# Six buffers for split weights, each 32 bytes further round a 128-byte block than the one before it

## Chip, cores and metric

The kernel runs on one core of one Trainium2 chip. The metric is device time in microseconds (us), the median of repeated executions. The engines are named as the profile names them: PE is TensorE (PEld its weight loads), DVE is VectorE, ACT is ScalarE, POOL is GpSimd, SP is SyncE.

## What is computed

Two transformer blocks of one sequence, 256 tokens by 1024 features, in float32. Cut to its calls:

```python
def reference(...):
    x = first_block(x, c, w_ada, ..., w_in, ..., w_branch, w_out, w_up, conv_w, conv_b, w_down)
    return second_block(x, gla_w_in_2, ..., gla_w_out_2, w_kv_2, swa_w_in_2, swa_w_out_2, ...)
    # first_block: modulation by c @ w_ada; three attention branches on h @ w_in, gated and
    #   merged through w_branch and w_out; conv FFN: gelu(conv(h @ w_up)) * gate, @ w_down
    # second_block: a gated linear attention layer (w_in, w_out), then shared keys and values
    #   (w_kv) and dilated window attention (swa_w_in, swa_w_out); layer norms around them
```

Nearly all the work is a product of a 256-row activation with a weight matrix of 1024 or more rows, and each weight is read from memory once.

## The kernel before

**Split weights.** A float32 product is made of three matmuls in the faster format float32r (`mm3`, L267): each operand is a high part and a low part, and low x high, high x low and high x high are added up. Activations are split where they are made. Weights are split as they arrive, by the class `Stream` (L100). It holds the list of all weight chunks in the order of their use. For each chunk one DMA of up to 128 x 2048 floats goes into one of three `raw` buffers (L144). Then, for each half of 1024 columns, ACT copies it in rounded form into `whi` (L154) and DVE subtracts that from the raw half into `wlo` (L155). There are six `whi` and six `wlo` buffers (HLB, L26), 4096 bytes in each partition, so three chunks' worth. `get` (L164) issues the chunk that is wanted and two more (LOOK). A buffer comes free when the last matmul on its half has read it.

**How the matmuls use them.** Most products (`wstat`, L512, called by `wpair`, L517; `branch`, L751) load 128 x 128 of the weights as the stationary operand and stream the activation's 256 columns. Products by token (`tokmm`, L793) do it the other way round: 128 tokens of the activation are loaded, and 512 columns of the weights stream. The engines' orders come out of a scheduling framework that keeps dependencies and gives a tile a buffer of its tag; `high_priority` and `issue_after` steer it.

**Placing.** `Lines` (L203) wraps a pool: a tile of less than 128 bytes goes into a separate small pool, and any other is rounded up to a multiple of 128 bytes, so that all larger tiles begin at the same place in a block of 128 bytes. The pool `wp` holds `raw`, `whi` and `wlo`; `cn` holds constants and long-lived tiles, among them `rbc` (L485, one value for each token, used by `first_h`, L411, in the first stage alone); `p0` is the pool of the first stage, closed at L504.

**Order around the weights.** In the list (L276 to L318) the branch weights `br` come between the gate weights `zg`: `("br", 2)`, `("zg", 11)`, then `("out", 0)` to `("out", 3)`. The second half of `("br", 2)` is still read after the matmuls of `("zg", 11)` (`branch2`, L755, called with 2 and 3 at L790), while `out` is already being fetched and split. `swa_scores` (L1248) keeps row statistics in `sst`, a small tile with four buffers, for each of its 16 blocks of 128 queries.

Of the kernel before, what the change touches and what calls it, by code (L numbers as in the profile page):

```python
# [8 lines left out]
F32 = mybir.dt.float32  # L9
F32R = mybir.dt.float32r  # L10
# [8 lines left out]
S = 256  # L19
# [6 lines left out]
RAWB, HLB, LOOK, LASTF = 3, 6, 2, 4  # L26
# [73 lines left out]
class Stream:  # L100


    def __init__(self, nc, pool, rawbufs, hlbufs, look):
        self.nc, self.pool, self.rawbufs, self.hlbufs, self.look = nc, pool, rawbufs, hlbufs, look
        self.items = []
        self.done = []
        self.pos = 0
        self.idx = {}
        self.behind = ()
        self.after = {}  # L110
        self.later = []
        self.pri = 0

    def also(self, key, ap, fn):

# [16 lines left out]
    def _chunk(self, i):  # L132
        nc = self.nc
        key, ap, n, part = self.items[i]
        if part < 0:
            raw = self.early.tile([128, n], F32, tag="early", name="early", bufs=3)
        else:
            raw = self._raw()
        if not part:
            for o in range(0, n, 1024):  # L140
                nc.sync.dma_start(raw[:, o:o + 1024], ap[:, o:o + 1024])
            self.done.append(raw)
            return
        nc.sync.dma_start(raw[:, :n], ap)  # L144
        parts = []
        for o in range(0, n, part) if part > 0 else range(0, -part, 1024):
            m = min(part, n - o) if part > 0 else min(1024, -part - o)
            hi = self.pool.tile([128, 1024], F32R, tag="whi", name="whi", bufs=self.hlbufs)
            lo = self.pool.tile([128, 1024], F32R, tag="wlo", name="wlo", bufs=self.hlbufs)
            with ExitStack() as st:  # L150
                for ins in self.behind:
                    st.enter_context(self.tc.issue_after(ins))
                st.enter_context(self.tc.high_priority(self.pri))
                i0 = nc.scalar.activation(hi[:, :m], raw[:, o:o + m], AF.Copy)  # L154
                i1 = nc.vector.tensor_sub(lo[:, :m], raw[:, o:o + m], hi[:, :m].bitcast(F32))  # L155
                self.last = (i0.ins, i1.ins)
            parts.append((hi, lo))
        self.done.append((part, parts) if part > 0 else (raw, (1024, parts)))
# [68 lines left out]
def hybrid_blocks(ctx, tc, A, out, dbg=None):  # L227
# [3 lines left out]
    cn = Lines(ctx.enter_context(tc.tile_pool(name="cn", bufs=1)), sm)  # L231
    wp = Lines(ctx.enter_context(tc.tile_pool(name="wp", bufs=1)))
    ps = ctx.enter_context(tc.tile_pool(name="ps", bufs=1, space=PSUM))

    def open_pool(name):
        st = ExitStack()
        p = st.enter_context(tc.tile_pool(name=name, bufs=1))
        return Lines(p, st.enter_context(tc.tile_pool(name=name + "s", bufs=1))), st.close

    p1a, close_p1a = open_pool("p1a")  # L240
    p0, close_p0 = open_pool("p0")
# [8 lines left out]
    def at_t():  # L250
        return ps.tile([128, 512], F32, tag="at", name="at", bufs=2)
# [5 lines left out]
    def mm(o, l, r, start, stop, share=False):  # L257
        return pe.matmul(o, l, r, start=start, stop=stop, skip_group_check=share)  # L258
# [16 lines left out]

    ws = Stream(nc, wp, RAWB, HLB, LOOK)  # L276
    ws.tc = tc
    for j in range(KK):
        ws.add(("ada", j), A["w_ada1"][j], 2048, 0)
        ws.add(("in1", j), A["w_in1"][j], 2048, -1536)  # L280
# [201 lines left out]
    pr = at_t()  # L482
    for b in range(2):
        mm(pr[:, b * 128:(b + 1) * 128], r1[:, b:b + 1].to_broadcast([128, 128]), ident, True, True)
    rbc = cn.tile([128, S], F32, name="rbc")  # L485
    dve.tensor_copy(rbc, pr[:, 0:S])
    h32, at = first_h(0, ga)
    for j in range(KK):
# [17 lines left out]
    wk = p1  # L506
# [396 lines left out]
    wk = p2  # L903
# [64 lines left out]
    wk = p3  # L968
# [245 lines left out]
    wk = p4  # L1214
# [33 lines left out]
    def swa_scores(h):  # L1248

        kv, q = h // 4, sq[h]  # L1250
        r = []
        for b in range(2):
            bs = slice(b * 128, (b + 1) * 128)
            pl = at_t()
            mm(pl[:, 0:256], q[:, 0, bs], skT[:, 0 + kv, :], True, True)
            mm(pl[:, 256:384], q[:, 1, bs], skT[:, 2 + kv, bs], True, True)
            mm(pl[:, 384:512], q[:, 2, bs], skT[:, 4 + kv, bs], True, True)
            P = wk.tile([128, 512], F32, name="sP", tag="sP", bufs=2)
            st = wk.tile([128, 4], F32, name="sst", tag="sst", bufs=4)
            dve.tensor_tensor_reduce(P, pl, swam[:, b, :], 1.0, -3e38, OP.add, OP.max, accum_out=st[:, 0:1])  # L1260
            dve.tensor_scalar(st[:, 1:2], st[:, 0:1], -SC_SWA, None, op0=OP.mult)
            act.activation(P, P, AF.Exp, scale=SC_SWA, bias=st[:, 1:2], accum_out=st[:, 2:3])
            dve.reciprocal(st[:, 3:4], st[:, 2:3])
            dve.tensor_scalar(P, P, st[:, 3:4], None, op0=OP.mult)
            r.append(P)
        return r
# [37 lines left out]
    for h in range(8):  # L1304
        if h < 7:
            swa_q0(h + 1)
        if h in (2, 4, 6):
            swa_pv(h // 2 - 1)
        if h == 7:
            pe = Queue(tc, pe, last_mm)  # L1310
            tokmm(y4, [(sact[3], 0, w, 1024)], 1024, False, False)
        Ps = swa_scores(h)
        if h == 2:
            lnb0 = row("lnb0", nc.scalar)
            x3p = p4.tile([128, 2, D], F32, name="x3p")
            x3v = x3d.rearrange("b p d -> (b p) d").rearrange("(i b a) d -> a b i d", b=4, a=4)
            for a in range(4):
                for b in range(4):
                    q = (a % 2) * 64 + b * 16
                    nc.scalar.dma_start(x3p[q:q + 16, a // 2, :], x3v[a, b])  # L1320
        if h == 6:
            lnr = row("lng1", nc.scalar), row("lnb1", nc.scalar)
        if h in (4, 5):
            dve.tensor_add(x3p[:, h - 4, :], x3p[:, h - 4, :], lnb0)
        if h < 7:
            swa_q1(h + 1)
        if h in (2, 6):
            w = ws.get(("sout", h // 4))
            for u in range(2 - h // 4):
                tokmm(y4, [(sact[h // 4 * 2 + u], 0, w, u * 1024)], 1024, h == 2 and u == 0, False)  # L1330
        if h < 7:
            swa_tr(h, Ps)
# [106 lines left out]
```

## Time and profile before

| What | Value |
|---|---|
| Median of 3 runs | 745.18 us |
| Lowest, highest | 742.55, 747.92 us |
| The profiled execution: its time | 743.82 us |
| its span, first to last instruction | 741.8 us |
| its mean granted clock of TensorE | 0.979 |
| Instructions | 12192 |
| PE busy | 711.8 us (96%) |
| DVE, ACT busy | 547.3 us (74%), 407.8 us (55%) |
| Moved by DMA | 148.74 MB, mean 201 GB/s |

The span runs from the first to the last instruction; some 2 us of the execution lie around it. A busy matmul engine is not one at its peak, since matmuls overlap; so the distance between their starts matters as well as their durations. The granted clock is the share of 2.4 GHz that TensorE was given, 0.50 being 1.2 GHz.

### The profile page before, as it was taken

The numbers are of one execution on the slowest core, as the hardware profiler recorded it, in microseconds if no ns is written. First come the engines' busy times: TensorE is split into PE (matmuls) and PEld (weight loads), VectorE is DVE, ScalarE is ACT, GpSimd is POOL, SyncE is SP. The second block draws the span as 40 slices with busy tenths as digits, with TensorE's granted clock in tenths as the row PEclk, the third lists the DMA queues.
The fourth block names the chain that finished last, engine by engine and source line by source line (L and its number), as shares of the span: only waits on it lengthen the run. The fifth ranks groups of instructions, "written<-read, shape, count | busy, mean of one in ns | idle before, by whom it ended". The sixth has DMA issues, their size and how long they took to land. (4 is left out here: it accounts for less than half of the span.)

```text
span 741.8 us, 12192 instructions
## 1 busy us (share of the span) xinstructions
PE 711.8 (96%) x4878; PEld 649.1 (88%) x4878; DVE 547.3 (74%) x933; ACT 407.8 (55%) x675; POOL 20.2 (3%) x34
## 2 busy tenths in 40 slices
PE   4999999999979999999999999999989999999995
PEld 4888888998869999998999797888879999999984
DVE  5877969898868676758655756675877679677866
ACT  3447788546548455554454685343555556555542
POOL 0001000000010000000000200001010000000000
PEclk8999999999998999999999999999999999999999
DMA  8995767567634764658545454331447755433201
GB/s 313 421 350 204 291 255 296 204 240 274 243 142 171 266 246 171 243 204 307 211 179 191 142 220 171 115 114 57 166 160 253 259 189 180 158 128 131 97 1 57
DMA packets 24600, 148.74 MB, mean 201 GB/s; under 512 B 2992, under 2 KB 3248, under 8 KB 9568
## 3 DMA queue, kind: packets, MB, share of 16 engines
q1 hardware_dynamic: 21888, 139.05, 51.1%
q0 software_dynamic: 1280, 5.18, 2.1%
q10 hardware_dynamic: 1376, 3.74, 1.5%
q8 instruction: 38, 0.62, 0.3%
q14 instruction: 18, 0.15, 0.1%
HBM read 145.86 MB, written 2.10 MB: 199 GB/s over the span
## 5 line engine op out<-in xcount | busy, mean ns | idle before, releaser
L155 DVE TENSOR_TENSOR wlo<-raw,whi 128x1024 fp32r<-128x1024 f32 (+1 forms) x193 | 231.4, 1210 | 67.7 <-ACT whi L154 67.6
L154 ACT ACTIVATE whi<-raw 128x1024 fp32r<-128x1024 f32 (+1 forms) x193 | 199.4, 1050 | 95.8 <-PE acc L258 41.7
L258 PE MATMUL mm<-h2hi,wlo 128*128 128x256 f32 x352 | 100.2, 286 | 0.0
L258 PE MATMUL mm<-h2hi,whi 128*128 128x256 f32 x352 | 100.0, 285 | 0.0
L258 PE MATMUL mm<-h2lo,whi 128*128 128x256 f32 x352 | 97.3, 283 | 0.0
L258 PE MATMUL mm<-x3hi,wlo 128*128 128x256 f32 x304 | 87.9, 290 | 0.0
L258 PE MATMUL mm<-x3hi,whi 128*128 128x256 f32 x304 | 87.0, 287 | 0.0
L258 PE MATMUL mm<-x3lo,whi 128*128 128x256 f32 x304 | 83.7, 283 | 0.0
L258 PEld LDWEIGHTS mm<-h2hi,wlo 128*128 128x128 f32 x352 | 68.5, 194 | 0.3
L258 PEld LDWEIGHTS mm<-h2hi,whi 128*128 128x128 f32 x352 | 68.4, 194 | 0.0
L258 PEld LDWEIGHTS mm<-h2lo,whi 128*128 128x128 f32 x352 | 66.5, 192 | 0.4
L258 PE MATMUL mm<-hhi,wlo 128*128 128x256 f32 x208 | 60.9, 293 | 0.0
L258 PE MATMUL mm<-hhi,whi 128*128 128x256 f32 x208 | 60.4, 291 | 0.0
L258 PE MATMUL mm<-hlo,whi 128*128 128x256 f32 x208 | 60.1, 289 | 0.0
L258 PEld LDWEIGHTS mm<-x3hi,wlo 128*128 128x128 f32 x304 | 59.2, 195 | 0.2
L258 PEld LDWEIGHTS mm<-x3hi,whi 128*128 128x128 f32 x304 | 59.2, 195 | 0.0
L258 PEld LDWEIGHTS mm<-x3lo,whi 128*128 128x128 f32 x304 | 57.4, 192 | 0.0
L258 PEld LDWEIGHTS mm<-hhi,wlo 128*128 128x128 f32 x208 | 40.6, 195 | 1.8 <-issue 0.9
L258 PEld LDWEIGHTS mm<-hlo,whi 128*128 128x128 f32 x208 | 40.6, 195 | 0.8 <-issue 0.8
L258 PEld LDWEIGHTS mm<-hhi,whi 128*128 128x128 f32 x208 | 40.5, 195 | 0.6 <-issue 0.5
L440 DVE SCALAR_TENSOR_TENSOR adacc<-raw,cact,adacc 128x1024 f32<-128x1024 f32 x28 | 35.7, 1275 | 0.2
L258 PE MATMUL acc<-whi,flo 128*128 128x512 f32 x88 | 34.8, 395 | 0.0
(355 smaller groups left out, 1609.8 us busy)
## 6 DMA issues: line engine op xcount, KB each, us to landing
raw<-in_w_up_dram SPq DMA_DIRECT2D x22, 1024.0 KB, 4.8
raw<-in_w_ada_dram SPq DMA_DIRECT2D x16, 1024.0 KB, 4.8
raw<-in_swa_q_dram SPq DMA_DIRECT2D x16, 1024.0 KB, 4.9
raw<-in_w_zg_dram SPq DMA_DIRECT2D x12, 1024.0 KB, 5.2
raw<-in_w_dn_dram SPq DMA_DIRECT2D x11, 1024.0 KB, 4.8
raw<-in_w_ada_dram SPq DMA_DIRECT2D x16, 512.0 KB, 8.6
early<-in_w_in_dram SPq DMA_DIRECT2D x8, 1024.0 KB, 7.5
raw<-in_gla_vg_dram SPq DMA_DIRECT2D x8, 1024.0 KB, 4.9
```

The costliest lines, as they stand in the source:

```text
L154: i0 = nc.scalar.activation(hi[:, :m], raw[:, o:o + m], AF.Copy)
L155: i1 = nc.vector.tensor_sub(lo[:, :m], raw[:, o:o + m], hi[:, :m].bitcast(F32))
L258: return pe.matmul(o, l, r, start=start, stop=stop, skip_group_check=share)
L440: dve.scalar_tensor_tensor(a, w, c, a, op0=OP.mult, op1=OP.add)
```

## The change

The six buffers of the high parts become six tags with one buffer each, `whi0` to `whi5`, likewise `wlo0` to `wlo5`, and a counter `made` gives them out in turn. Ahead of everything else in `wp`, a loop allocates for each tag its buffer and behind it a pad of four floats, past the rounding of `Lines`. Two further edits give space: `rbc` moves from `cn` to `p0`, and `sst` has three buffers instead of four.

```diff
@@ class Stream
-        self.pri = 0
+        self.pri = self.made = 0
@@ _chunk
-            hi = self.pool.tile([128, 1024], F32R, tag="whi", name="whi", bufs=self.hlbufs)
-            lo = self.pool.tile([128, 1024], F32R, tag="wlo", name="wlo", bufs=self.hlbufs)
+            j = self.made % self.hlbufs
+            self.made += 1
+            hi = self.pool.tile([128, 1024], F32R, tag=f"whi{j}", name="whi")
+            lo = self.pool.tile([128, 1024], F32R, tag=f"wlo{j}", name="wlo")
@@ hybrid_blocks
     ws.tc = tc
+    for part in ("whi", "wlo"):
+        for j in range(HLB):
+            wp.pool.tile([128, 1024], F32R, tag=f"{part}{j}", name="home")
+            wp.pool.tile([128, 4], F32, tag=f"{part}pad{j}", name="pad")
@@
-    rbc = cn.tile([128, S], F32, name="rbc")
+    rbc = p0.tile([128, S], F32, name="rbc")
@@ swa_scores
-            st = wk.tile([128, 4], F32, name="sst", tag="sst", bufs=4)
+            st = wk.tile([128, 4], F32, name="sst", tag="sst", bufs=3)
```

## Rows read from the trace of the kernel before

**Rows 1.** The page, part 1: busy us (share of the span) x instructions.
```profile
PE 711.8 (96%) x4878; PEld 649.1 (88%) x4878; DVE 547.3 (74%) x933; ACT 407.8 (55%) x675; POOL 20.2 (3%) x34
```

**Rows 2.** Windows: us, busy of PE, PEld, DVE, ACT, POOL; clock; DMA.
```profile
223.50:417.00 193.50, 192.09 (x1342) 179.84 (x1341) 133.87 (x183) 101.30 (x149) 2.21 (x4) 0.99 0.58 210
...
550.00:712.00 162.00, 161.97 (x1230) 156.27 (x1229) 125.23 (x216) 96.03 (x152) 1.13 (x2) 0.99 0.48 167
```

**Rows 3.** Waits of PE: us in total, times, longest; first and last of twelve.
```profile
PE acc L885 <- DVE x L189: 4.1, 3, 2.7
...
PE at L690 <- ACT Pat L674: 0.2, 1, 0.2
```

**Rows 4.** Waits of all engines: us in total, times, longest; those of the splits.
```profile
DVE wlo L155 <- ACT whi L154: 68.1, 71, 2.7
...
ACT whi L154 <- PE acc L258: 41.7, 36, 3.1
```

**Rows 5.** Timeline of PE at 300 and 200 us: start, duration, instruction.
```profile
300.10 0.28 PE L258 MATMUL mm<-h2lo,whi 128*128 128x256 f32 x1
...
301.06 0.28 PE L258 MATMUL mm<-h2hi,wlo 128*128 128x256 f32 x1
...
199.68 0.39 PE L258 MATMUL acc<-whi,mlo 128*128 128x512 f32 x1
...
201.94 0.39 PE L258 MATMUL acc<-wlo,mhi 128*128 128x512 f32 x1
```

**Rows 6.** Timeline of PE shortly after 224 us, eight starts apart.
```profile
224.19 0.41 PE L258 MATMUL mm<-h2hi,wlo 128*128 128x256 f32 x1
...
225.90 0.41 PE L258 MATMUL mm<-h2hi,wlo 128*128 128x256 f32 x1
```

**Rows 7.** Windows as above: granted clock at 224 us and at 300 us.
```profile
223.60:225.00 1.40, 1.40 (x8) 1.40 (x7) 1.40 (x4) 1.40 (x5) 0.00 (x0) 0.50 0.00 0
...
300.00:301.20 1.20, 1.20 (x13) 1.20 (x12) 1.20 (x2) 0.00 (x0) 0.00 (x0) 1.00 0.10 41
```

**Rows 8.** Timeline of PE's weight loads: one at 300 us; eight behind one another.
```profile
300.10 0.19 PEld L258 LDWEIGHTS mm<-h2hi,whi 128*128 128x128 f32 x1
...
461.79 0.97 PEld L258 LDWEIGHTS at<-Xq,Xk 128*128 128x128 f32 x8
```

**Rows 9.** Windows, whole span: tile whi (PE, PEld, DVE, ACT), then tile wlo (without ACT).
```profile
0.00:741.80 741.80, 573.31 (x2720) 444.72 (x2720) 245.96 (x209) 211.94 (x209) 0.98 0.55 201
...
0.00:741.80 741.80, 422.16 (x1360) 263.21 (x1360) 245.96 (x209) 0.98 0.55 201
```

**Rows 10.** Groups by form, DVE: count | busy us, mean ns | idle before.
```profile
L935 DVE SCALAR_TENSOR_TENSOR u<-mm,cols,u 128x255 f32<-128x255 f32 x22 | 10.6, 483 | 16.4 <-ACT u L934 16.3
...
L189 DVE SCALAR_TENSOR_TENSOR h2lo<-acc,sh,h2hi 128x256 fp32r<-128x256 f32 x8 | 3.2, 477 | 1.7 <-ACT h2hi L189 1.7
```

**Rows 11.** Tile whi, ACT: duration min/median/max, first and last start; whole, 225 to 230.5.
```profile
L154 ACT ACTIVATE whi<-raw x193: 833/1058/1107, 63.0 to 711.4; 128x1024 fp32r<-128x1024 f32 x185, 128x768 fp32r<-128x768 f32 x8
...
L154 ACT ACTIVATE whi<-raw x5: 1098/1100/1107, 225.6 to 229.4; 128x1024 fp32r<-128x1024 f32 x5
```

**Rows 12.** Timelines of ACT and PE around the start of the product by w_out.
```profile
188.43 1.06 ACT L154 ACTIVATE whi<-raw 128x1024 fp32r<-128x1024 f32 x1 [2.67 <-PE mm L258]
...
195.04 1.04 ACT L154 ACTIVATE whi<-raw 128x1024 fp32r<-128x1024 f32 x1
...
194.54 0.28 PE L258 MATMUL mm<-yhi,whi 128*128 128x256 f32 x1
```

**Rows 13.** Tiles rbc and sst: duration min/median/max in ns, first and last start.
```profile
L413 DVE TENSOR_TENSOR xT<-xT,rbc x8: 414/418/425, 15.9 to 22.9; 128x256 f32<-128x256 f32 x8
...
L1260 DVE DVE_READ_ACCUMULATOR2_ANT sst<- x16: 80/83/85, 605.0 to 719.3; 128x1 f32 x16
...
L1264 DVE TENSOR_SCALAR sP<-sP,sst x16: 477/487/491, 607.8 to 720.6; 128x512 f32<-128x512 f32 x16
```

## Prediction

> **What bounds the kernel now.** I read the page's first part, then busy time by stage, then the waits, then the matmuls one by one. TensorE (PE) is busy 711.8 of the 741.8 us [rows 1]. In the two long stages it is busy 192.09 of 193.50 us and 161.97 of 162.00 us [rows 2], so there the time is simply the number of matmuls times the distance from one start to the next; I call that distance the pitch. What PE does wait for is short: twelve rows from 4.1 us down to 0.2 us, and in none does a matmul wait for a high or low part of the weights [rows 3]. The splitting engines stand the other way round: the ScalarE (ACT) split that makes `whi` waits for PE to give a buffer back, 41.7 us in 36 waits behind one kind of matmul, and the VectorE (DVE) split that makes `wlo` waits for ACT [rows 4]. The buffers are full and their makers idle. So the change moves the end only through the pitch, or through a wait that it creates.
>
> **The pitch.** At 300 us eight matmuls of 256 columns start in 301.06 - 300.10 = 0.96 us: 120 ns each. Ten of 512 columns start in 201.94 - 199.68 = 2.26 us: 226 ns [rows 5]. The 256 further columns cost 106 ns, so a matmul costs about 13 ns besides its columns. Shortly after 224 us, where the granted clock is 0.50 (the 1.2 GHz level; it is 1.00, 2.4 GHz, at 300 us [rows 7]), eight of the same 256-column matmuls take 225.90 - 224.19 = 1.71 us, 214 ns each [rows 6]. That is 2 x 107, with no 13 ns on top. So at full clock the 13 ns belong to a step ahead of the array that does not halve with its clock: getting an operand started, by all that can be seen. A weight load starts in the same hundredth of a us as the matmul before it, at 300.10 [rows 5, 8]. Where loads set the pace, eight in a row, the pitch is (0.97 - 0.19)/7 = 111 ns [rows 8]. Under a 256-column matmul a load therefore has 120 - 111 = 9 ns of cover.
>
> **The change, part by part.**
>
> *Six tags and pads instead of one tag.* Nothing is executed for the homes and pads; no instruction is added or removed. A pad of four floats follows each home, and if it takes 32 bytes the high parts lie at 0, 32, 64, 96, 0, 32 bytes in a block of 128, and the low parts, six pads further on, at 64, 96, 0, 32, 64, 96. Before, `Lines` rounds every row to 128 bytes and all lie at 0. Twelve pads are 384 bytes, three blocks, so `raw`, allocated behind them, keeps its place in a block, and no DMA changes.
>
> *DVE on shifted buffers.* The trace has a near case: L935 works on `u` shifted by 4 bytes, 255 columns in 483 ns, while the aligned `h2lo` with the same kind of pointer operand takes 477 ns for 256 [rows 10]. A shift costs at most some 6 ns; on 209 low splits that is 1.3 us, on an engine whose splits nobody waits for. Cost 0; 1.3 us if all of it were exposed.
>
> *ACT on shifted buffers.* The trace shows no shifted ACT split. From below: the 1024-column split has a median of 1058 ns, and five run to 1098 to 1107 ns between 225.6 and 230.5 us, where DVE splits beside it [rows 11]. If that is two engines in the same place of a block, the shift gives back 5 x 45 ns = 0.2 us there. From above: one split 50 ns longer each time is 209 x 0.05 = 10.5 us of ACT time, spread over an engine that stands waiting for buffers 41.7 us behind one releaser alone [rows 4]. Both ends are hidden by the full buffers: 0. If that cover were gone, the 10.5 us would count.
>
> The Trainium skill, "SBUF — State Buffer", section "Who interferes with whom", says that only the port pair shared by VectorE and GpSimd causes contention and that PE and ACT wait for nobody. By that rule, staggering has nothing to give. The slow ACT splits beside DVE [rows 11] do not fit it well; by the rule the sum is 0, by those rows 0.2 us off the path.
>
> *PE on shifted buffers.* 2720 matmuls use `whi` and 1360 `wlo` [rows 9]. `tokmm` uses the weights as the moving operand: 12 matmuls for each half of out (8), dn (22), gvg (16), gout (8), kvv (8) and sout (8), 70 halves, 840 matmuls, 560 on `whi` and 280 on `wlo`. The other 4080 - 840 = 3240 load them as the stationary operand (2160 and 1080). By the offsets 4 of 6 `whi` and 5 of 6 `wlo` buffers leave place 0: 373 + 233 = 606 moving and 1440 + 900 = 2340 stationary matmuls. No row shows one on a buffer off place 0, so bounds. From above: a shifted operand pays one more start of 13 ns. Moving: 606 x 13.3 = 8.1 us. Stationary: 13.3 ns less 9 ns of cover, 4.3 ns, x 2340 = 10.1 us. From below: if the 13 ns are a collision of the load and the stream starting together at the same place, the shift removes it: 9 ns (down to the loads' 111) x 2340 = 21.1 us and 8.1 us of the moving. I take 0: the 13 ns are the same for a short and a long stream [rows 5], which is how a fixed start looks, and a stream and a load that read at different rates pass each other's place in the block wherever they begin.
>
> *Fixed turns.* One tag gave a tile whichever slot came free; six tags force strict turns. They differ in one place. The second half of out1 comes six halves after the second half of br2, which is read until 194.54 us; before, its split ran at 188.43 us, so it sat in another slot [rows 12]. Now it must wait until about 194.8 us, some 6 us later, changing places with the split at 195.04. Queued behind it on ACT and DVE are only the splits of out2. PE reaches that half after 34 more matmuls of 226 ns, at 194.7 + 7.7 = 202.4 us; split there by 195.04 + 1.06 + 1.22 = 197.3 us, it is 5 us early. `raw` of out1 comes free 6 us later too, for a weight that is not needed before 223 us. Cost 0; with the cover gone, 6 us less 5, about 1 us.
>
> *`rbc` moved, `sst` from 4 to 3.* `rbc` has its last of eight reads at 22.9 us [rows 13], long before `p0` closes after the first stage. The 16 score blocks are spread from 605.0 to 719.3 us, about 7 us each, and `sst` is last read by L1264, 2.8 us after its block's start [rows 13]; a slot used again three blocks later never waits. Cost 0.
>
> **Sum.** 0 on the profiled execution's 743.82 us (span 741.8 and 2.0 around it). That execution lies 1.4 us below the median of the three runs, 745.18, well inside their 742.55 to 747.92. I forecast the median: 745.2 us.
>
> **Rivals.**
>
> *A shifted operand costs PE a start (slower).* Place: moving weights first, from `out` to the last `sout`. Price: 745.2 + 8.1 = 753.3 us, and 763.4 us with the stationary 10.1 us. It decides once a shifted load grows by over 9 ns, or a shifted stream at all. For: PE has no slack [rows 2], so any of it shows in full. Against: nothing in the trace shows PE at odds with an address. The same page of the Trainium skill, section "Specifications (TRN2)", puts the penalty on crossing 16-byte lines; by that rule a shift by a multiple of 32 crosses no more of them, and this rival gives 745.2 us.
>
> *Collision relieved (faster).* 745.2 - 29.2 = 716.0 us, if the 13 ns are a collision between the load and the stream, or part of that. For: both begin at the same instant at the same place [rows 5, 8]. Against: the reasons above.
>
> *A new wait at out1.* 745.2 + 1 us at most: within no change.
>
> *It does not do what it says.* If a pad takes a whole block, all buffers stay at place 0, only the turns change: 745.2 us, 5 in 100, within no change.
>
> **How the numbers follow.** A run of this kernel can tell about 1% from no change, 737.7 to 752.6 us. Zero by rows everywhere, with the new wait and the empty change: 63 in 100. The shifted start: 22 in 100, about two thirds of it at 753 to 758 (moving operands, or part of the loads). The relieved collision: 15 in 100. A range from 738 to 758 us leaves out most of the faster case and the upper third of the slower, some 2 in 10; the likeliest case's own range is 741 to 750 us. Faster 0.15, same 0.63, slower 0.22.
>
> **What would show it.** If right: pitches of 120 and 226 ns as before, loads 111 ns apart where they set the pace, PE about 712 us busy, the split of out1's second half near 195 us with no PE wait behind it, ACT splits at 225 us no longer near 1.1 us or unchanged, with no effect either way. The slower rival shows a pitch near 240 ns in `tokmm`, on some buffers and not on others; the faster one a pitch near 111 ns. Wrong would be any PE wait for `whi` or `wlo`, or splits so long that the buffers run empty.

## The result and the profile after

The changed kernel takes 753.76 us (median of 4 runs, 751.94 to 758.5); the kernel before, timed beside it, 745.1 us (4 runs, 742.55 to 747.92). The ratio is 1.0135, with a 95% interval of 1.0104 to 1.0165: slower by a little over 1%. The profiled execution took 753.55 us, of which the span is 751.5 us; before, the span was 741.8 us.

The page of the changed kernel, part 1 (busy us, share of the span, instructions), answers to [rows 1]:

```profile
PE 711.3 (95%) x4878; PEld 646.7 (86%) x4878; DVE 547.6 (73%) x933; ACT 408.2 (54%) x675; POOL 20.1 (3%) x34
```

Taken together, the work itself did not get longer. Every engine has the instruction counts of before, and PE is busy 711.3 us against 711.8 (the pitches did move, in both directions; see below). So the 9.7 us of longer span are time in which PE waits. The waits of PE after (engine, line and tile that wait, what for: us in total, times, longest) answer to [rows 3]:

```profile
PE acc L891 <- DVE x L191: 7.3, 3, 4.7
PE acc L891 <- DVE xr L191: 4.4, 1, 4.4
...
PE mm L260 <- DVE st L678: 3.5, 1, 3.5
...
PE acc L891 <- ACT xr L191: 2.1, 1, 2.1
...
PE mm L260 <- DVE x2lo L191: 0.9, 1, 0.9
PE at L191 <- DVE sg L191: 0.8, 1, 0.8
```

The top row was 4.1 us [rows 3], and the second stood at 3.1 us. The wait put down to `st` is new. L891 is the transposes at the end of a stage: the residual is added, normalised (L191 is the helper's line) and transposed, and only then can the matmuls of the next stage begin. I call such a place a join. There are three large ones: into the FFN, into the gated linear attention (GLA), and into the shared keys and values. I measure a join from the start of the last matmul of the output product to the start of the first matmul of the next stage.

Windows of the kernel before: us from and to, length, then busy us of PE, PEld, DVE, ACT and POOL (instructions in brackets), granted clock, DMA share, GB/s. The first three are the joins, the others what lies around them (the FFN, between the first and the second join, is left out):

```profile
215.77:223.61 7.84, 3.27 (x18) 2.46 (x17) 5.30 (x11) 5.41 (x14) 2.38 (x3) 0.74 0.00 0
413.12:417.14 4.02, 2.61 (x19) 1.76 (x17) 2.25 (x5) 1.34 (x4) 0.54 (x1) 1.00 0.00 0
545.05:550.34 5.29, 2.49 (x18) 1.77 (x17) 3.42 (x9) 1.77 (x4) 0.56 (x1) 1.00 0.27 84
67.51:215.77 148.26, 146.79 (x1093) 133.74 (x1092) 125.69 (x250) 95.32 (x196) 3.16 (x5) 0.99 0.70 258
417.14:545.05 127.91, 125.99 (x717) 108.66 (x716) 86.97 (x127) 69.87 (x103) 5.92 (x8) 0.99 0.42 154
550.34:741.80 191.46, 183.27 (x1343) 174.24 (x1342) 143.76 (x259) 103.65 (x166) 2.67 (x4) 0.98 0.42 147
```

The same windows after:

```profile
217.58:227.35 9.77, 3.28 (x18) 2.46 (x17) 7.38 (x13) 7.07 (x16) 2.31 (x3) 0.70 0.23 78
417.00:422.20 5.20, 2.61 (x18) 1.75 (x16) 5.01 (x7) 3.21 (x7) 0.54 (x1) 1.00 0.30 93
553.72:561.64 7.92, 3.10 (x18) 2.53 (x17) 5.53 (x12) 3.92 (x7) 0.55 (x1) 0.86 0.41 123
66.54:217.58 151.04, 145.71 (x1093) 132.95 (x1092) 125.90 (x250) 95.87 (x197) 3.22 (x6) 0.98 0.69 253
422.20:553.72 131.52, 128.15 (x717) 109.54 (x716) 84.27 (x125) 67.29 (x101) 5.92 (x8) 0.97 0.41 146
561.64:751.50 189.86, 181.18 (x1344) 171.76 (x1342) 141.36 (x257) 101.38 (x163) 2.67 (x4) 0.99 0.42 145
```

The balance, after less before: up to the gates -0.97 us (66.54 - 67.51), gates to output product +2.78, join +1.93, FFN +0.14 (189.65 against 189.51), join +1.18, GLA +3.61, join +2.63, rest -1.60. Together 9.70 us. The three joins alone make +5.74 us. In each of them DVE and ACT now execute more instructions, the first with DVE 13 instead of 11 and ACT 16 instead of 14, and DMA is busier than before; in the first two it had stood still. What has come in? Timelines of ACT and DVE at the first join, before (start, duration, instruction, idle time ahead of it):

```profile
225.59 2.06 ACT L154 ACTIVATE whi<-raw 128x1024 fp32r<-128x1024 f32 x2
...
216.98 0.21 DVE L189 TENSOR_SCALAR ms<-ssr 128x1 f32<-128x1 f32 x1
...
220.20 0.21 DVE L189 TENSOR_SCALAR ms<-ssr 128x1 f32<-128x1 f32 x1 [0.34 <-ACT junk L189]
```

And after:

```profile
217.80 1.05 ACT L156 ACTIVATE whi<-raw 128x1024 fp32r<-128x1024 f32 x1
...
220.54 1.05 ACT L156 ACTIVATE whi<-raw 128x1024 fp32r<-128x1024 f32 x1
...
218.88 1.23 DVE L157 TENSOR_TENSOR wlo<-raw,whi 128x1024 fp32r<-128x1024 f32 x1 [0.25 <-ACT whi L156]
220.02 0.21 DVE L191 TENSOR_SCALAR ms<-ssr 128x1 f32<-128x1 f32 x1
...
222.81 1.22 DVE L157 TENSOR_TENSOR wlo<-raw,whi 128x1024 fp32r<-128x1024 f32 x1
223.95 0.21 DVE L191 TENSOR_SCALAR ms<-ssr 128x1 f32<-128x1 f32 x1
```

Two splits of weights that no matmul wants yet stand between the steps of the normalisation. Before, the first split came at 225.59 us, behind the whole join. Counted from the last output matmul (215.77 and 217.58 us), the small step `ms` after the first `wlo` split moves from 1.21 to 2.44 us, the one after the second from 4.43 to 6.37 us. The last of these differences is 1.94 us, and the join is 1.93 us longer. The first split adds 1.23 us, its own length; the second adds 0.71 us, less than its length, in part because the step that it holds up had an idle 0.34 us ahead of it before.

The instruction lists of the two programs say the same for the whole kernel. In the kernel before, the 209 halves are split in the order of the list on both engines. In the changed one the order on ACT runs, around the first join, 57, 60, 61, 58, 59 (58 and 59 are a chunk of `up`, 60 and 61 the next one), around the second 122, 125, 126, 127, 123, 124, within GLA 148, 151, 152, 149, 150, and around the last join 156, 159, 160, 158, 157. Each time the chunk that is overtaken is the one that the kernel holds back with `ws.behind` (L930, L969, L1153, L1208 of the changed kernel): `get` gives that order to the first chunk issued after a join and then clears it. So one tag had done a second job. Splits of one tag kept the order of the list, and holding back one chunk held back all behind it.

The lists show two more differences. In the attention branches some chunks have their two halves swapped: DVE, for one, makes the low part of half 23 before that of half 22, though PE reads 22 first. And PE's own list differs in 205 places, all in the attention branches and at the start of GLA, none in a join. So in the joins the splits alone have moved; elsewhere the splits and PE's own order changed together, and no run parts the two in general.

The swap explains the new wait. PE, the changed kernel:

```profile
89.36 0.55 PE L260 MATMUL mm<-hhi,wlo 128*128 128x256 f32 x1 [3.54 <-DVE st L678]
```

DVE there, first half 23, then half 22:

```profile
84.83 1.22 DVE L157 TENSOR_TENSOR wlo<-raw,whi 128x1024 fp32r<-128x1024 f32 x1
...
87.99 1.22 DVE L157 TENSOR_TENSOR wlo<-raw,whi 128x1024 fp32r<-128x1024 f32 x1
```

By the lists this matmul is the first that reads half 22, and up to it PE's list is that of before. The low part of half 22 is finished at 89.21 us and the matmul starts 0.15 us later; in the kernel before, half 22 came first, at 85.37 us, and PE did not wait. The profile names `st` because that short instruction ended between the two, but the matmul does not read it: PE waits for `wlo`.

### The profile page after: what moved, and what is told of

It reads as the page before. It is cut to its first block, busy times and chain, and to the rows that moved or that the text cites. A ratio compares the mean times of both kernels' runs of the same rounds, so it can differ in the third digit from the quotient of the medians.

```text
span 751.5 us, 12210 instructions
## 1 busy us (share of the span) xinstructions
PE 711.3 (95%) x4878; PEld 646.7 (86%) x4878; DVE 547.6 (73%) x933; ACT 408.2 (54%) x675; POOL 20.1 (3%) x34
## 5 line engine op out<-in xcount | busy, mean ns | idle before, releaser
L260 PE MATMUL mm<-x3hi,whi 128*128 128x256 f32 x304 | 85.3, 282 | 0.0
```

## Experiments

**Theories.** *Order*: the separate tags let splits slip into the joins, and the places cost nothing. *Address*: operands at shifted places make PE's matmuls or loads start later; this is the slower rival of the prediction, whose 753.3 us lies close to what was measured. Every kernel was timed beside the kernel before; the ratio is to that. All keep the two edits on `rbc` and `sst`, and compute everything.

### One tag, shifted places

```diff
 # the kernel before, with rbc in p0 and three sst
-            hi = self.pool.tile([128, 1024], F32R, tag="whi", name="whi", bufs=self.hlbufs)
+            hi = self.pool.pool.tile([128, 1032], F32R, tag="whi", name="whi", bufs=self.hlbufs)[:, :1024]
 # lo likewise
```

> Keeps one tag with six buffers for the high parts and one for the low parts, as the kernel before, but each buffer is 1032 floats long of which 1024 are used, so that neighbours lie 32 bytes further round, as in the changed kernel. The instructions of every engine stand in the order of the kernel before. Order theory (six tags let later splits slip between the operations of the four transitions, and the shift itself costs nothing): 742 to 746 us, the step from the last output matmul of the first stage to the last transpose of the FFN's input stays near 7.8 us; if the shift also changes the pitches as in the changed kernel (256-column matmuls 118 ns, 512-column 232 ns) the end is nearer 742. Address theory (operands at shifted places make TensorE's matmuls or loads start later): 753 to 755 us, as the changed kernel.

Measured: 742.91 us, ratio 0.9974 (0.9950 to 0.9998). The address theory falls: the same 32-byte steps with the old order are not slower. The first join takes 7.84 us, as before.

### Six tags, no shift

```diff
 # the changed kernel
-            wp.pool.tile([128, 4], F32, tag=f"{part}pad{j}", name="pad")
```

> The changed kernel without the pads: six tags of one buffer each, all at the same place in the block of 128 bytes. The instructions of every engine stand in the order of the changed kernel. Order theory: 753 to 758 us, with the splits of two later halves again between the operations of the transition into the FFN and that step at 9 to 10 us; the pitches are again 120 and 227 ns if those came from the shift. Address theory: 745 us.

Measured: 754.72 us, ratio 1.0131 (1.0099 to 1.0164), the ratio of the changed kernel itself. Its windows over the three joins, columns as above:

```profile
216.10:225.98 9.88, 3.63 (x18) 2.66 (x17) 7.48 (x13) 7.18 (x16) 2.38 (x3) 0.67 0.23 79
415.96:421.42 5.46, 2.83 (x19) 2.03 (x17) 5.24 (x7) 3.47 (x7) 0.66 (x2) 0.95 0.34 108
550.46:558.38 7.92, 3.10 (x18) 2.53 (x17) 5.53 (x12) 3.93 (x7) 0.55 (x1) 0.72 0.40 121
```

Long joins with the same extra instructions, and no buffer shifted. The whole loss comes with the tags.

### Room only

```diff
 # the kernel before
-    rbc = cn.tile([128, S], F32, name="rbc")
+    rbc = p0.tile([128, S], F32, name="rbc")
-            st = wk.tile([128, 4], F32, name="sst", tag="sst", bufs=4)
+            st = wk.tile([128, 4], F32, name="sst", tag="sst", bufs=3)
```

> The kernel before with only the edits that make room: three buffers for the small transposed state instead of four and the broadcast rows in the other pool. Both theories: 744 to 746 us, no change. If it is over 750 us, the room and neither the tags nor the places is what costs.

Measured: 744.58 us, ratio 1.0000 (0.9980 to 1.0019). These two edits cost nothing.

### Six tags and pads, splits in turn

```diff
 # the changed kernel; ACT's split, DVE's likewise with self.last[1]
+                with ExitStack() as turn:
+                    if self.made > 1:
+                        turn.enter_context(self.tc.issue_after(self.last[0]))
-                i0 = nc.scalar.activation(hi[:, :m], raw[:, o:o + m], AF.Copy)
+                    i0 = nc.scalar.activation(hi[:, :m], raw[:, o:o + m], AF.Copy)
```

> The changed kernel, pads and all, with each split told to stand behind the split made before it on its engine; nearly all instructions then stand in the order of the kernel before (ten of VectorE and five of ScalarE around the second half of the first output weight stand elsewhere). Order theory: the loss is gone, 742 to 746 us. Address theory: 753 to 755 us, as the changed kernel, since the places are the same.

Measured: 742.91 us, ratio 0.9972 (0.9949 to 0.9995). The buffers, tags and places are those of the changed kernel; the order alone is put back, and with it the loss is gone. Its windows over the joins and its waits there:

```profile
214.47:222.31 7.84, 3.28 (x19) 2.46 (x17) 5.20 (x11) 5.30 (x14) 2.31 (x3) 0.76 0.00 0
411.33:415.34 4.01, 2.60 (x18) 1.76 (x17) 2.25 (x5) 1.34 (x4) 0.54 (x1) 1.00 0.00 0
543.04:548.34 5.30, 2.50 (x19) 1.78 (x17) 3.42 (x9) 1.77 (x4) 0.55 (x1) 1.00 0.23 84
```

```profile
PE acc L897 <- DVE x L197: 4.1, 3, 2.7
...
PE acc L897 <- DVE xr L197: 3.1, 1, 3.1
```

Lengths, instruction counts and waits are those of before. This kernel also has the one change of turns that the prediction had found: ACT splits the second half of out1 at 193.29 us, where the kernel before did at 188.43 [rows 12], and no matmul of the output product waits for it.

### In turn at the joins only, and everywhere else only

```diff
 # as above, and where the buffers are made:
+            if self.behind:
+                self.joined = self.made
-                    if self.made > 1:
+                    if self.made > 1 and self.made - self.joined < 10:
 # the other kernel: >= 10
```

`behind` is also set once for each of the eight chunks of the first stage (L496), so its splits count with the joins.

> The changed kernel, six tags and pads, where only the first ten splits that follow a chunk held behind a stage's last operations are told to stand behind the split made before them; the other splits are free. Order theory, loss at the joins of stages: 742 to 747 us, nearly all of the loss is gone. Rival, loss spread over all splits that changed places (above all among the gates of the first stage): 748 to 752 us, at most half of it is gone. Address theory: 753 us.

> The complement: all splits are told to stand in turn but for the first ten behind each join, which are free. Loss at the joins: 751 to 756 us, as the changed kernel. Loss spread over all splits: 746 to 750 us.

Measured: in turn behind the joins 742.8 us, ratio 0.9981 (0.9955 to 1.0007); everywhere else 753.04 us, ratio 1.0119 (1.0082 to 1.0156). The ten splits after each hold decide. The rest don't show in the time, though they cost PE one wait of 1.7 us in the first of the two kernels, for the low part of half 38, which DVE makes there behind that of 39. The waits of PE in the second kernel:

```profile
PE acc L900 <- DVE x L200: 7.3, 3, 4.7
PE mm L269 <- DVE st L687: 4.4, 1, 4.4
PE acc L900 <- DVE xr L200: 3.9, 1, 3.9
```

The wait put down to `st` is there too, at 86 us, between the first and the second attention branch, and so is the swap of halves 22 and 23. Three kernels have this swap, and in each the matmul starts 0.15 us after the end of half 22's low part: the changed kernel waits 3.5 us, this one 4.4, and the one with six tags and no shift 2.0, where the profile names another instruction (`th` of ACT). Where half 22 is first, the wait is absent or 0.5 us, but for the run below: it has 1.8 us, with half 22 late because ACT's split waited 2.70 us for the weight's DMA. So the swap makes the wait, and its length depends on the DMA too.

### Free at one join

```diff
 # the kernel in turn everywhere else, with
-            if self.behind:
+            if self.behind and key[0] == "up":
                 self.joined = self.made
```

> The changed kernel with all splits in turn but for the first ten behind one join, that into the FFN. Loss at the joins: the two gaps of TensorE between the transposes of the FFN's input grow from 4.6 us together to 6.5 us, nothing else moves, 744 to 746 us where all in turn gave 742.9. If a single join costs nothing by itself: 742 to 743.5 us and gaps of 4.6 us.

The window over the first join, and DVE within it:

```profile
218.36:228.13 9.77, 3.95 (x18) 3.17 (x17) 7.37 (x13) 7.07 (x16) 2.31 (x3) 0.63 0.22 70
```

```profile
219.66 1.23 DVE L166 TENSOR_TENSOR wlo<-raw,whi 128x1024 fp32r<-128x1024 f32 x1 [0.25 <-ACT whi L162]
...
223.60 1.22 DVE L166 TENSOR_TENSOR wlo<-raw,whi 128x1024 fp32r<-128x1024 f32 x1
```

The join is 9.77 us long, to the hundredth that of the changed kernel, and the join into GLA stays at 4.02 us. So two early splits cost their own join 1.93 us. The two largest gaps within it add up to 5.8 us, not the 6.5 us that I expected; PE's matmuls there fill the rest more slowly (clock 0.63). The whole kernel took 744.22 us, ratio 0.9998 (0.9970 to 1.0025), against 0.9972 with all in turn: in the expected direction, but the intervals overlap, so the price of this one join stands on the window and not on the total.

### What the shift does by itself

The pitch did change with the shift. Means of the distance from one matmul's start to the next, over all neighbouring pairs of one kind in each trace (pairs over 150 or 250 ns apart left out, which removes gaps and the half clock):

| Kernel | weights loaded, 256 columns | weights streamed, 512 columns | ratio of time |
|---|---|---|---|
| before | 119.9 ns | 228.1 ns | 1 |
| room only | 119.9 | 228.2 | 1.0000 |
| six tags, no shift | 119.9 | 228.2 | 1.0131 |
| changed kernel | 118.2 | 231.8 | 1.0135 |
| one tag, shifted | 118.4 | 231.4 | 0.9974 |
| six tags, shifted, in turn | 118.2 | 231.8 | 0.9972 |

Four runs asked what of the place does it. Two put each piece at a place by its use, in buffers of 1048 floats:

```diff
 # six tags, splits in turn; homes of 1048 floats, no pads
+            turn = key[0] not in ("out", "dn", "gvg", "gout", "kvv", "sout")
+            p = 8 * ((j * turn + j) % 4)
+            q = 8 * ((j * turn + 2 * turn + j + 2) % 4)
+            hi = self.pool.pool.tile([128, 1048], F32R, tag=f"whi{j}", name="whi")[:, p:p + 1024]
+            lo = self.pool.pool.tile([128, 1048], F32R, tag=f"wlo{j}", name="wlo")[:, q:q + 1024]
 # the other kernel: key[0] in (...)
```

> Six tags, splits in turn, 1048 floats to a buffer, and each piece put at a place chosen by its use: the pieces that TensorE loads as weights (256-column matmuls) get the shift of 32 bytes from neighbour to neighbour, the pieces that it streams (512-column matmuls) all begin at place 0. If the shift shortens the pitch where pieces are loaded (119.9 to 118.2 ns in the runs so far) and lengthens it where they are streamed (228.2 to 231.6 ns): 3240 loaded pieces give some 5 us and the streamed ones lose nothing, 738 to 741 us. If the pitches are only a matter of how the profile models ends of matmuls, or are given back in waits: 742 to 745 us.

> The reverse: only the pieces that TensorE streams are shifted, the loaded ones begin at place 0. If the pitches decide: some 840 matmuls by 3.4 ns, 3 us more than without any shift, 746 to 749 us, with pitches of 119.9 and 231 ns. If they do not: 742 to 745 us.

Measured: loaded pieces shifted 742.0 us, ratio 0.9983 (0.9962 to 1.0004); streamed pieces shifted 743.93 us, ratio 1.0019 (0.9995 to 1.0044). Neither gave the pitches that I expected. With all streamed pieces at place 0 their pitch was 231.0 ns all the same, and with all loaded pieces at place 0 theirs was 119.0 ns. So a piece's own place in the block of 128 bytes sets at most about 1 ns of its pitch: the shifted pieces have 118.3 ns in the first of these kernels and 232.1 ns in the second. What both kernels share is that most neighbours are no longer 4096 bytes apart. So the last two:

```diff
 # six tags, splits in turn: no pads at all; or pads of 128 bytes
-            wp.pool.tile([128, 4], F32, tag=f"{part}pad{j}", name="pad")
+            if part == "whi" or j < 3:
+                wp.pool.tile([128, 32], F32, tag=f"{part}pad{j}", name="pad")
```

> Six tags, splits in turn, no pads: all buffers at place 0 and 4096 bytes from neighbour to neighbour; every engine's order is that of the run with pads and splits in turn. Expected pitches as in the kernel before (119.9 ns where pieces are loaded, 228.1 ns where they are streamed) and 743 to 746 us: the shift by itself is worth about 2 us of 745.

> The same with pads of 128 bytes instead of 32 (behind all six buffers of the high parts and three of the low ones): all buffers still at place 0 of the block of 128 bytes, but 4224 bytes from neighbour to neighbour instead of 4096. If the place in the block sets the pitches: 119.9 and 228.1 ns, as without pads, 743 to 746 us. If it is that neighbours are no longer 4096 bytes apart: 118 to 119 and 231 to 232 ns, as with pads of 32 bytes, 741 to 744 us.

Measured: without pads 744.85 us, ratio 0.9999 (0.9973 to 1.0025), pitches 119.9 and 228.1 ns; with pads of 128 bytes 745.49 us, ratio 1.0009 (0.9984 to 1.0033), 119.1 and 231.1 ns. Matmuls that stream `wlo` in the FFN, by tile (count: duration ns min/median/max, first and last start), without pads and then with them:

```profile
L266 PE MATMUL acc<-wlo,fhi x88: 389/389/398, 243.9 to 414.4; 128*128 128x512 f32 x88
```

```profile
L266 PE MATMUL acc<-wlo,fhi x88: 387/393/404, 241.3 to 412.0; 128*128 128x512 f32 x88
```

All operands are at place 0 in both, and the order of every engine is the same. Yet the steady 389 ns spreads to 387 to 404 ns once neighbours are 4224 bytes apart (the last three of the low parts stay at 4096). So addresses matter to the pitch beyond the place in the block. I take it to be the distance between the buffers, but that is not shown: the pads also move what is allocated behind them, `raw` and `fhi` among it, by 1152 bytes. The run was not faster, though its pitches lie near those of the two shifted kernels at 0.997. Whether the shift is worth 0.2 to 0.3% stays open: two intervals exclude no change by a hair, three others that hold shifted pieces (0.9981, 0.9983, 1.0019) do not.

## Why the prediction was right or wrong

**The forecast of no change was wrong**: 753.8 us against 745.2. That the measured time lies in the range of 738 to 758 us, and next to the slower rival's 753.3 us, is luck: the upper part of the range was there for that rival, and its mechanism is refuted by the first and the fourth run.

**"Fixed turns" is the step that failed.** It said that one tag gives a tile whichever slot comes free, that six tags force strict turns, and that "they differ in one place", at a cost of 0, 1 us at most. That compared when a buffer is free. It left out what the tag did to the order of the instructions: with one tag a later split stood behind an earlier one, also one that was being held back; with six it need not. The place that it named, out1, is real and harmless. The places that cost were others. Where `ws.behind` holds a chunk back, the three joins are longer by 5.74 us, and in GLA PE waits 0.8 us for `sg`. Ahead of the output product, the swapped halves 22 and 23 make PE wait 3.5 us, more than the whole +2.78 us there. Another part of the +3.61 us in GLA is clock: it is 0.56 (the 1.2 GHz level) for the first 7.80 us of the stage and was 0.78 in the mean over its first 7.86 us before, as these two windows show, before and then after:

```profile
417.14:425.00 7.86, 7.52 (x51) 7.32 (x50) 7.02 (x8) 7.79 (x10) 3.32 (x5) 0.78 0.76 256
```

```profile
422.20:430.00 7.80, 6.83 (x30) 6.12 (x29) 5.28 (x7) 4.51 (x7) 3.32 (x5) 0.56 0.86 308
```

PE issued 30 matmuls there instead of 51. The last stage gives 1.60 us back. How much clock a join costs differs between the profiles of kernels with the same order (the kernel with six tags and no shift had 0.82 over 7.78 us at this place), so these two terms belong to this profile; the joins themselves repeat to 0.3 us in the three kernels that have the changed order throughout or behind all holds. Where a join has the old order, the first takes 7.48 to 7.85 us, the second 4.01 to 4.02 and the last 5.29 to 5.91, so up to 0.6 us of the +2.63 at the last join may be its own spread.

**"The change moves the end only through the pitch, or through a wait that it creates"** was right, and the sign listed against the forecast, any PE wait for `whi` or `wlo`, did come: the 3.5 us at 86 us. The prediction took the full buffers as cover for every split; they are none for a half that is made behind its neighbour. The larger loss came from another side, where I did not look: a split that is *early* takes DVE and ACT from the chain that everything waits for. "Cover" was counted for the splits and not for the work beside which they run.

**PE on shifted buffers**, priced at 0 between -29.2 and +18.2 us: the value was nearly right by luck, the reasons were not. There is an effect, of both signs, which nearly cancels: about 1.7 ns off 3240 matmuls is 5.5 us, 3.6 ns on 840 is 3.0 us, a gain of some 2.5 us by this estimate; 0.26 and 0.28% were measured in the two runs with all places shifted and the old order. Neither "one more start of 13 ns" nor a collision that the shift removes is seen; the signs named for the two rivals (240 and 111 ns) did not appear.

The rule cited there, from "SBUF — State Buffer" in the Trainium skill, section "Who interferes with whom" (only the shared port pair causes contention), gives no place for a pitch that depends on where the buffers lie. Here the pitches moved by -0.8 and +3.0 ns with every operand at the same place in its block; which partner, if any, PE meets there no run shows. By the penalty for crossing 16-byte lines, from the same page of the Trainium skill, section "Specifications (TRN2)", steps of 32 bytes lose nothing, and the first run agrees: 0.9974.

**DVE and ACT on shifted buffers**, 0: right. The splits, groups by form (count | busy us, mean ns | idle before), before and then after:

```profile
L155 DVE TENSOR_TENSOR wlo<-raw,whi 128x1024 fp32r<-128x1024 f32 x185 | 223.8, 1221 | 67.4 <-ACT whi L154 67.4
```

```profile
L157 DVE TENSOR_TENSOR wlo<-raw,whi 128x1024 fp32r<-128x1024 f32 x185 | 224.9, 1221 | 70.4 <-ACT whi L156 70.4
L156 ACT ACTIVATE whi<-raw 128x1024 fp32r<-128x1024 f32 x185 | 193.9, 1059 | 99.2 <-PE acc L260 47.3 <-PE mm L260 36.0 <-DMA raw<-in_w_br_dram 4.5
```

ACT's median over all its raw splits moved from 1058 [rows 11] to 1060 ns; the three between 229.3 and 232.4 us, beside DVE, still have a median of 1.10 us, so the shift gave nothing back there.

**`rbc` and `sst`**, 0: right, 1.0000 when done alone.

## What to carry to other kernels

When buffers of one tag are split into several tags, compare the instruction order of every engine before and after: the tag may have been what kept look-ahead work out of a critical chain and in the order in which it is read, and a hold on one chunk may have rested on it. An early piece of hidden work isn't free if it runs on the engine that carries the chain; here 1.2 us of it, twice in a join, cost the join 1.9 us. To keep the new placing, write the old order down as well, which took this kernel from 1.0135 to 0.9972.

## What was not expected of the hardware

The pitch of matmuls whose weights lie in buffers exactly 4096 bytes apart is steady (119.9 and 228.1 ns in the mean). With 4128 bytes, or 4224 for most of them, 256-column matmuls that load the weights come at 118.2 to 119.1 ns and 512-column ones that stream them at 231.1 to 231.8 ns. The place of the piece within 128 bytes decides at most about 1 ns of it. The cause stays open, whether it is the distance or another consequence of the addresses, and so does whether the time gains by it.
